# A hybrid decoder layer on one core: eight orders of products in the expert layer, and three smaller reorderings

## The chip, the cores and the metric

One core of one Trainium2 chip. The metric is the device time of the program in microseconds (us); lower is better.

## What the kernel must compute

One decoder layer for 256 tokens of width 1024 in fp32, followed by a final RMSNorm:

```python
for l in range(DEPTH):                       # DEPTH = 1
    h = rmsnorm(x, norm_mix_g[l])
    proj = h @ w_in[l]                       # q, k, v, gu, gv, gate_a, gate_b
    y_a = moba_attention(q, k, v) @ moba_w_proj[l]
    y_b = gmlp_spatial_gating(gu, gv, ...) @ gmlp_w_proj[l]
    x = x + (sigmoid(gate_a) * y_a + sigmoid(gate_b) * y_b) @ w_out[l]
    x = x + memory_cross_attention(rmsnorm(x, norm_xa_g[l]), rmsnorm(mem, norm_mem_g[l]), ...)
    x = x + peer_ffn(rmsnorm(x, norm_ffn_g[l]), w_q, subkeys, w_down, w_up)
return rmsnorm(x, final_g)
```

`peer_ffn` scores each token against 2 x 128 sub-keys for each of 8 heads, takes the best 16 pairs, and adds up, with softmax weights, gelu(h . w_down[e]) * w_up[e] for the experts e that were chosen, out of 128 x 128.

## The kernel before

Every fp32 weight block (128 x 1024) is loaded by SyncE, rounded by ScalarE to a high part `hi` (L140), and the rest, the low part `lw`, is subtracted by VectorE or GpSimd (L142; `lo_engine` says which). Blocks that are listed in `spread` have their subtraction cut into two halves (L146), which are put into a list `half` and emitted where the program calls `half.pop(0)()`. A product is three matmuls: high weights by high data, high weights by low data, low weights by high data (`mm3`, L179 to L181). Loads and conversions run ahead of use: taking a block converts the one two places later.

The order of work on each engine is the order in which the program emits it. The front part runs the mixing block, the cross attention (`xquery`, `xscore`, `xscale`, `xtrans`, `xvalue`; transposes at L641) and its output projection. Then 16 query blocks follow (`for n in range(16)`): each is a `tblock` of 24 matmuls, a copy to `qp`, and one block later `pscore` (L752), a score copy to `S`, and `best`, a round of top-8 operations on VectorE. In the first three of them `pq.add` squares the residual stream on ScalarE and adds up on VectorE (L267); `pq.matmul` (L273) sums over partitions, in the middle of block 3; `newton` makes the third norm's factor, `bcast` spreads it, and `norm_block` normalises one eighth of the data in each of eight blocks.

The expert layer computes all 16,384 experts densely. `down` (128 calls) makes one block of 128 experts' first-layer products, 24 matmuls of 256 columns into the accumulator `A`, and a gelu. VectorE chooses the experts meanwhile (routing: the top-8 rounds and many small operations); one-hot products (`gstep`, tile `m`) then spread the routing weights, and `umm` (L1012 to L1016) multiplies with the second layer's blocks, matmuls of 512 columns. A plan at the top interleaves `down`, `gstep` and `umm`. The final norm squares the accumulators on ScalarE (L1082), forms the factor in small steps, scales on GpSimd (first 128 tokens) or VectorE (last 128) and stores each half row.

Of the kernel before, what the change touches and what calls it, by code (L numbers as in the profile page):

```python
# [16 lines left out]
F32 = mybir.dt.float32  # L17
# [4 lines left out]
AF = mybir.ActivationFunctionType  # L22
OP = mybir.AluOpType
# [3 lines left out]
D = 1024  # L27
S = 256
KD = 8
EPS = 1e-6  # L30
# [15 lines left out]
N_XO, N_PQ = 4, 16  # L46
# [43 lines left out]
def body(tc, I, out, dbg=None):  # L90
# [3 lines left out]
    V, A, P, T, SY = nc.vector, nc.scalar, nc.gpsimd, nc.tensor, nc.sync  # L94
# [10 lines left out]
    nf = I["wf"].shape[0]  # L105
    steps = plan()
    stream = [("f", n) for n in range(nf)] + [x for x in steps if x[0] in "du"]
    raws, convs, later = {}, {}, []
    spread, half = [*range(52, 60), nf - N_PQ - 3, *range(nf - N_PQ - 2, nf - N_PQ + 2)], []
    pos = {"load": 0, "conv": 0, "take": 0}  # L110

    def load_to(n):
        while pos["load"] < min(n, len(stream)):
            m = pos["load"]
            kind, idx = stream[m]
            raw = wst.tile([128, 1024], F32, name="raw", bufs=RAW)
            SY.dma_start(raw, {"f": I["wf"], "d": I["wd"], "u": I["wu"]}[kind][idx])
            raws[m] = raw
            pos["load"] += 1

    def lo_engine(m):
        kind, idx = stream[m]
        if kind == "f":
            return V if idx < nf - N_PQ + 2 else P
        if kind == "d" and idx < FIRST:
            return P
        return V
# [23 lines left out]
    def take(kind):  # L151
        m = pos["take"]
        assert stream[m][0] == kind
        pos["take"] += 1
        conv_to(m + 1 + LEAD)
        load_to(m + 1 + LEAD + RAW)
        for fn in later:
            fn()
        later.clear()
        return convs.pop(m)  # L160


    def sl(k):
        return (slice(None), k, slice(None))

    def tsl(t):
        return slice(t * 128, (t + 1) * 128)
# [9 lines left out]
    def mm3(ps, w, wsl, x, xsl, start, stop):  # L177
        (wh, wl), (xh, xl) = w, x
        T.matmul(ps, wh[wsl], xh[xsl], start=start, stop=False)  # L179
        T.matmul(ps, wh[wsl], xl[xsl], start=False, stop=False)  # L180
        T.matmul(ps, wl[wsl], xh[xsl], start=False, stop=stop)  # L181
# [14 lines left out]
    def mean_sq(v, ms, width):  # L196
        V.tensor_scalar(v, ms, 1.0 / width, EPS, op0=OP.mult, op1=OP.add)
# [5 lines left out]
    mid = ctx.enter_context(tc.tile_pool(name="mid", bufs=1))  # L203
# [10 lines left out]
    def pmm():  # L214
        return pf.tile([128, S], F32, name="mm", bufs=3)
# [7 lines left out]
    xT = fo.tile([128, KD, S], F32, name="xT")  # L223
# [5 lines left out]
    raw0 = wst.tile([128, 1024], F32, name="raw", bufs=RAW)  # L229
    raws[0] = raw0  # L230
    pos["load"] = 1
    for k in range(2):
        SY.dma_start(raw0[:, k * 512:(k + 1) * 512], I["wf"][0][:, k * 512:(k + 1) * 512])
        SY.dma_start(xT[:, k], I["xT"][:, k])
    for j in range(1, 4):
        SY.dma_start(xT[:, 2 * j:2 * j + 2], I["xT"][:, 2 * j:2 * j + 2])
        load_to(j + 1)
    warm = cst.tile([128, 1], F32, name="warm")
    A.activation(warm, ones, AF.Sqrt)
    wps = pat([128, 128])  # L240
# [48 lines left out]
    def tblock(w, x, n=KD, base=0, mid=None):  # L289
        ps = pmm()  # L290
        for k in range(n):
            if mid and k == n // 2:
                mid()
            c = (base + k) * 128
            mm3(ps, w, (slice(None), slice(c, c + 128)), x, sl(k), k == 0, k == n - 1)
        return ps
# [23 lines left out]
    raw0 = raws.pop(0)  # L320
# [7 lines left out]
    for k in range(2):  # L328
        ks = slice(k * 512, (k + 1) * 512)
# [48 lines left out]
    for c in range(4):  # L378
        for nm in ("q", "k"):
            first = c == 0  # L380
            ps = tblock(take("f"), xg, mid=(sqp.matmul if nm == "q" else rope_norm) if first else None)
# [139 lines left out]
    for c in range(4):  # L521
        ps = tblock(take("f"), xg)
# [37 lines left out]
    for c in range(4):  # L560
        ps = tblock(take("f"), mg)
# [42 lines left out]
    pq = Squares(fp2, "x1")  # L604
    for c in range(KD):
        ps = tblock(take("f"), mp)
# [30 lines left out]
    def xtrans(t, h):  # L637
        ps = pat([128, 2, 2, 128])
        for i in range(2):
            for sb in range(2):  # L640
                T.transpose(ps[:, i, sb], Px[t][:, h + i, sb * 128:(sb + 1) * 128], ident)  # L641
        PT = fp2.tile([128, 2, 2, 128], F32, name="PT", bufs=4)
        if t:
            V.tensor_copy(PT, ps)
        else:
            A.copy(PT, ps)
        XT_[t, h] = PT


    def xscale(h):  # L650
        xr = fp2.tile([128, 2], F32, name="xr", bufs=4)
        V.reciprocal(xr, xs[:, :, 2, h])
        for t in range(2):
            V.tensor_scalar(Px[t][:, h], Px[t][:, h], xr[:, t:t + 1], None, op0=OP.mult)
# [26 lines left out]
    xscale(2)  # L681
    xtrans(0, 0)
    xtrans(1, 0)
    skh = [fo.tile([128, 8, 128], F32, name="kT")]
    P.dma_start(skh[0], I["skT"][:, 0:8])
    xscale(3)
    nm_.step()
    V.tensor_scalar(vm[:, 0], nm_.ps[0], rm[:, 0:1], None, op0=OP.mult)
    A.activation(vm[:, 1], nm_.ps[1], AF.Copy, scale=rm[:, 1:2])
# [8 lines left out]
    xg2 = pair("xg", fo)  # L698
    rp = rs1.enter_context(tc.tile_pool(name="route", bufs=2, side="right", reuse_waits="tile"))
    S1 = rp.tile([128, 8, 2, 2, 128], F32, name="S1", bufs=1)  # L700
    x2T = rp.tile([128, KD, S], F32, name="x2T", bufs=1)
    pq = Squares(fp2, "x2")
    for c2 in range(4):
        w = take("f")
        for c in range(2):
            cc = 2 * c2 + c
            ps = tblock(w, oxT, n=4, base=4 * c)
# [30 lines left out]
    h3 = pair("mg", mid)  # L738

    def norm_block(k):  # L740
        hx = fp2.tile([128, S], F32, name="hx", bufs=3)
        V.scalar_tensor_tensor(hx, x2T[:, k], gcol[:, 3, k:k + 1], r3bc, op0=OP.mult, op1=OP.mult)
        later.append(lambda: split(h3[0][:, k], h3[1][:, k], hx))
# [12 lines left out]
    for n in range(16):  # L756
        sk = skh[n // 8][:, n % 8]
        w = take("f")
        if n == 4:
            v3 = fp2.tile([128, 2], F32, name="v3")  # L760
            sq_sum(pq, v3)
        if n == 5:
            r3 = newton(fp2, v3, 2, "r3")
            V.tensor_copy(r3c, r3)
        ps = tblock(w, xg2, mid=pq.matmul if n == 3 else None)
        qp = fp2.tile([128, S], F32, name="qp", bufs=2)
        A.copy(qp, ps)
        qps[n] = (qp, sk)
        if n < 3:
            for k in range(3 * n, min(3 * n + 3, 8)):  # L770
                pq.add(x2T[:, k], A, V)
        if n == 7:
            bcast(r3, r3bc)
            norm_block(0)
        if 8 <= n < 15:
            norm_block(n - 7)
        if n > 0:
            pscore(n - 1)
    pscore(15)
# [6 lines left out]
    gp = g.enter_context(tc.tile_pool(name="exp", bufs=2, reuse_waits="tile"))  # L786
    pp = g.enter_context(tc.tile_pool(name="pexp", bufs=1, space=PSUM, reuse_waits="tile"))
    yps = [[pp.tile([128, 512], F32, name=f"y{t}{z}") for z in range(2)] for t in range(2)]
    Aq = {}

    def mblock():
        return pp.tile([128, 512], F32, name="m", bufs=2)

    def down(i2):
        w = take("d")
        ps = pp.tile([128, S], F32, name="A", bufs=2)
        for k in range(KD):
            mm3(ps, w, (slice(None), slice(k * 128, k * 128 + 128)), h3, sl(k), k == 0, k == KD - 1)
        a = gp.tile([128, S], F32, name="aring", bufs=RING)
        A.activation(a, ps, AF.Gelu_apprx_tanh)  # L800
        Aq[i2] = a
# [76 lines left out]
    n, spent = 0, 0.0  # L878
# [39 lines left out]
    for j in range(3):  # L918
        ps = mblock()[:, :S]
# [11 lines left out]
    for t in range(2):  # L931
        for k in range(KD):
            T.matmul(yps[t][k // 4][:, (k % 4) * 128:(k % 4 + 1) * 128], x2T[:, k, tsl(t)], ident,
                     start=(k % 4 == 0), stop=False, skip_group_check=True)
# [97 lines left out]
    for n, x in enumerate(rest):  # L1032
# [16 lines left out]
        else:  # L1049
            up_a(x[1])  # L1050
            up_b(x[1])
            w = take("u")
# [18 lines left out]
    sqs = wst.tile([128, D], F32, name="raw", bufs=RAW)  # L1071
    for t in range(2):
        ulast(ws, [UP[i2] for i2 in range(128 - TAILN, 128)], t)
        scale = P.tensor_scalar if t == 0 else V.tensor_scalar
        fs = gp.tile([128, 2], F32, name="fs")
        yg = wst.tile([128, D], F32, name="raw", bufs=RAW)
        fm = gp.tile([128, 1], F32, name="fm")
        fv = gp.tile([128, 1], F32, name="fv")
        sq = gp.tile([128, 1], F32, name="fsq")
        for z in range(2):  # L1080
            zs = slice(z * 512, (z + 1) * 512)
            A.activation(sqs[:, zs], yps[t][z], AF.Square, accum_out=fs[:, z:z + 1])  # L1082
            if z == 1:
                V.tensor_add(fm, fs[:, 0:1], fs[:, 1:2])
                mean_sq(fv, fm, D)
                A.activation(sq, fv, AF.Sqrt)
            V.tensor_mul(yg[:, zs], yps[t][z], fg[:, zs])
        fy = gp.tile([128, 1], F32, name="fy")
        V.reciprocal(fy, sq)
        fu = gp.tile([128, 1], F32, name="fu")  # L1090
        V.scalar_tensor_tensor(fu, fy, fy, fv, op0=OP.mult, op1=OP.mult)
        V.tensor_scalar(fu, fu, -0.5, 1.5, op0=OP.mult, op1=OP.add)
        for z in range(2):
            zs = slice(z * 512, (z + 1) * 512)
            scale(yg[:, zs], yg[:, zs], fy, fu, op0=OP.mult, op1=OP.mult)
            (SY if z == 0 or t == 0 else A).dma_start(out[0, tsl(t), zs], yg[:, zs])
    g.close()
    ctx.close()

# [73 lines left out]
```

## Time and profile before

| | us |
|---|---|
| median of 3 runs | 1051.2 (1049.24 to 1052.67) |
| profiled execution, its own time | 1049.31 |
| its span, first to last instruction | 1047.6 |
| TensorE matmuls busy | 1029.6 (98%) |
| VectorE busy | 763.3 (73%) |
| ScalarE busy | 593.9 (57%) |
| GpSimd busy | 63.5 (6%) |
| mean granted TensorE clock | 0.996 of full speed |

Times in the profile count from the span's start. Matmul records overlap, since they are pipelined: the distance from start to start is what one costs, not its own duration. In the profile PE is TensorE, DVE VectorE, ACT ScalarE, POOL GpSimd and SP SyncE.

### The profile page before, as it was taken

To read this page: it belongs to the slowest core of one execution; us is meant where nothing else is said; L and a number is where in the kernel's file an instruction comes from. 1 tells how busy PE (TensorE), PEld (TensorE's weight loads), DVE (VectorE), ACT (ScalarE), POOL (GpSimd) and SP (SyncE) were. 2 spreads that over 40 slices of the span, in tenths; PEclk is the share of its full clock that TensorE was granted. 3 is DMA by queue.
4 is the path that set the end of the run, shared out by engine and by line. 5 is a ranking of instruction groups with operands and counts; after the bars stand their busy time and mean duration, and the time that the engine had idled before them with its cause. 6 is when DMAs were issued, how large, how long until landed. Compare 5 with 4: busy or idle time off the path is not lost.

```text
span 1047.6 us, 19742 instructions
## 1 busy us (share of the span) xinstructions
PE 1029.6 (98%) x7862; PEld 953.1 (91%) x7862; DVE 763.3 (73%) x1502; ACT 593.9 (57%) x935; POOL 63.5 (6%) x53
## 2 busy tenths in 40 slices
PE   9999999998999999999999999999999999999997
PEld 7989999998999999999988998899999988888885
DVE  6765797688999899965656565666799766666666
ACT  6955745665654567755454545454678654444554
POOL 0400000016740000000000000000000000000000
PEclk9999999999999999999999999999999999999999
DMA  8644655554456534456666566656444565656562
GB/s 291 232 138 133 197 173 168 174 164 140 157 165 203 171 118 155 147 180 189 194 188 194 185 198 187 195 185 198 149 157 140 181 192 191 196 188 197 187 198 101
DMA packets 52365, 185.84 MB, mean 177 GB/s; under 512 B 5937, under 2 KB 6833, under 8 KB 52145
## 3 DMA queue, kind: packets, MB, share of 16 engines
q1 hardware_dynamic: 51552, 183.20, 54.6%
q8 instruction: 61, 1.00, 0.4%
q0 software_dynamic: 288, 1.05, 0.3%
q10 hardware_dynamic: 432, 0.34, 0.1%
q14 instruction: 32, 0.25, 0.1%
HBM read 183.52 MB, written 1.05 MB: 176 GB/s over the span
## 4 chain that ended last, share of the span: by engine, by line
PE 89%; DVE 7%; ACT 2%; DMA 1%; issue 1%; DVEq 0%; SPq 0%; ACTq 0%
PE A L179 11%; PE y L1016 11%; PE y L1013 11%; PE y L1012 11%; PE A L181 11%; PE A L180 11%; PE mm L179 5%; PE mm L180 5%; PE mm L181 5%; PE m L985 2%; PE m L984 2%; DVE lw L142 1%; ACT hi L140 1%; DMA raw<-in_wf 1%; PE at L406 1%; PE nat L312 1%
## 5 line engine op out<-in xcount | busy, mean ns | idle before, releaser
L142 DVE TENSOR_TENSOR lw<-raw,hi 128x1024 fp32r<-128x1024 f32 (+1 forms) x309 | 377.1, 1222 | 229.9 <-ACT hi L140 229.0
L140 ACT CAST hi<-raw 128x1024 fp32r<-128x1024 f32 (+1 forms) x341 | 355.4, 1043 | 189.4 <-issue 139.5
L179 PE MATMUL A<-mgh,hi 128*128 128x256 f32 x1024 | 290.2, 283 | 0.0
L181 PE MATMUL A<-mgh,lw 128*128 128x256 f32 x1024 | 287.6, 281 | 1.8 <-DVE lw L142 1.8
L180 PE MATMUL A<-mgl,hi 128*128 128x256 f32 x1024 | 287.4, 281 | 0.0
L181 PEld LDWEIGHTS A<-mgh,lw 128*128 128x128 f32 x1024 | 195.8, 191 | 2.2 <-DVE lw L142 2.2
L1012 PE MATMUL y<-hi,gahl 128*128 128x512 f32 x504 | 196.1, 389 | 0.0
L1013 PE MATMUL y<-lw,gahl 128*128 128x512 f32 x504 | 196.1, 389 | 0.0
L180 PEld LDWEIGHTS A<-mgl,hi 128*128 128x128 f32 x1024 | 192.8, 188 | 2.2
L179 PEld LDWEIGHTS A<-mgh,hi 128*128 128x128 f32 x1024 | 192.3, 188 | 2.2
L1016 PE MATMUL y<-hi,gahl 128*128 128x512 f32 x504 | 155.2, 389 | 0.0
L800 ACT ACTIVATE aring<-A 128x256 f32<-128x256 f32 x128 | 49.2, 384 | 161.7 <-PE A L181 161.7
L179 PE MATMUL mm<-xgh,hi 128*128 128x256 f32 x416 | 119.1, 286 | 0.3 <-DVE q L368 0.3
L181 PE MATMUL mm<-xgh,lw 128*128 128x256 f32 x416 | 116.4, 280 | 0.0
L180 PE MATMUL mm<-xgl,hi 128*128 128x256 f32 x416 | 116.4, 280 | 0.0
L1016 PEld LDWEIGHTS y<-hi,gahl 128*128 128x128 f32 x504 | 94.6, 188 | 19.6
L1012 PEld LDWEIGHTS y<-hi,gahl 128*128 128x128 f32 x504 | 94.6, 188 | 17.4
L1013 PEld LDWEIGHTS y<-lw,gahl 128*128 128x128 f32 x504 | 94.6, 188 | 17.4
L179 PEld LDWEIGHTS mm<-xgh,hi 128*128 128x128 f32 x416 | 79.0, 190 | 1.3 <-issue 0.7
L181 PEld LDWEIGHTS mm<-xgh,lw 128*128 128x128 f32 x416 | 79.1, 190 | 0.0
L180 PEld LDWEIGHTS mm<-xgl,hi 128*128 128x128 f32 x416 | 78.9, 190 | 0.1
L986 ACT ACTIVATE G<-m 128x512 f32<-128x512 f32 x64 | 66.0, 1141 | 5.0 <-PE m L985 2.3
(272 smaller groups left out, 1246.8 us busy)
## 6 DMA issues: line engine op xcount, KB each, us to landing
raw<-in_wd SPq DMA_DIRECT2D x128, 512.0 KB, 3.8
raw<-in_wu SPq DMA_DIRECT2D x128, 512.0 KB, 4.1
raw<-in_wf SPq DMA_DIRECT2D x83, 512.0 KB, 3.7
memT<-in_memT SPq DMA_DIRECT2D x1, 1024.0 KB, 7.3
xT<-in_xT SPq DMA_DIRECT2D x3, 256.0 KB, 6.7
out_y<-raw SPq DMA_DIRECT2D x3, 256.0 KB, 2.0
raw<-in_wf SPq DMA_DIRECT2D x2, 256.0 KB, 3.5
wmT<-in_wsT SPq DMA_DIRECT2D x1, 512.0 KB, 6.2
```

Source lines behind the costliest of these rows:

```text
L140: A.copy(hi[:, ps], raw[:, ps])
L142: lo_engine(m).tensor_sub(lw[:, ps], raw[:, ps], hi[:, ps].bitcast(F32))
L179: T.matmul(ps, wh[wsl], xh[xsl], start=start, stop=False)
L180: T.matmul(ps, wh[wsl], xl[xsl], start=False, stop=False)
L181: T.matmul(ps, wl[wsl], xh[xsl], start=False, stop=stop)
L800: A.activation(a, ps, AF.Gelu_apprx_tanh)
L984: T.matmul(ps[:, t], a1[at], bh[at], start=True, stop=False)
L985: T.matmul(ps[:, t], a1[at], bl[at], start=False, stop=True)
L986: A.activation(Gq[q][:, :, s * TG + c:s * TG + c + 8].rearrange("p i t -> p t i"), ps, AF.Copy, scale=1.0 / 16384.0)
L1012: T.matmul(yps[t][z], gh[:, tsl(t)], wh[:, zs], start=False, stop=False, skip_group_check=True)
L1013: T.matmul(yps[t][z], gh[:, tsl(t)], wl[:, zs], start=False, stop=False, skip_group_check=True)
L1016: T.matmul(yps[t][z], gl[:, tsl(t)], wh[:, zs], start=False, stop=False, skip_group_check=True)
```

## The change

Four edits. `down` takes one of eight orders by block number modulo 8: the old order; low weights first (1); low data first (2); the eight k-tiles backwards (3); the second matmul cut into 240 and 16 columns (4), or into 128 and 128 (5); all products with high weights before all with low (6); even k-tiles, then odd (7). The third norm's squares are spread 4, 3, 1 over the query blocks in place of 3, 3, 2, its column sums stand behind block 3 and not within it, the normalisation starts at block 6 and not 7, and two more low-part subtractions of query blocks go to VectorE; one more block before them is cut in halves, emitted within the cross attention. The first loads go in eight issues and not ten. The final norm forms mean and root in one ScalarE instruction and splits the last scaling between two engines.

```diff
-    spread, half = [*range(52, 60), nf - N_PQ - 3, *range(nf - N_PQ - 2, nf - N_PQ + 2)], []
+    spread, half = [*range(52, 60), nf - N_PQ - 4, nf - N_PQ - 3, *range(nf - N_PQ - 2, nf - N_PQ + 2)], []
...
-            return V if idx < nf - N_PQ + 2 else P
+            return V if idx < nf - N_PQ + 4 else P
...
-    for k in range(2):
-        SY.dma_start(raw0[:, k * 512:(k + 1) * 512], I["wf"][0][:, k * 512:(k + 1) * 512])
-        SY.dma_start(xT[:, k], I["xT"][:, k])
-    for j in range(1, 4):
-        SY.dma_start(xT[:, 2 * j:2 * j + 2], I["xT"][:, 2 * j:2 * j + 2])
-        load_to(j + 1)
+    SY.dma_start(raw0[:, 0:512], I["wf"][0][:, 0:512])
+    SY.dma_start(xT[:, 0:2], I["xT"][:, 0:2])
+    SY.dma_start(raw0[:, 512:1024], I["wf"][0][:, 512:1024])
+    SY.dma_start(xT[:, 2:4], I["xT"][:, 2:4])
+    load_to(2)
+    SY.dma_start(xT[:, 4:8], I["xT"][:, 4:8])
+    load_to(4)
...
     xtrans(1, 0)
+    half.pop(0)()
...
     xscale(3)
+    half.pop(0)()
...
-        ps = tblock(w, xg2, mid=pq.matmul if n == 3 else None)
+        ps = tblock(w, xg2)
...
-        if n < 3:
-            for k in range(3 * n, min(3 * n + 3, 8)):
-                pq.add(x2T[:, k], A, V)
-        if n == 7:
+        for k in ((0, 1, 2, 3), (4, 5, 6), (7,))[n] if n < 3 else ():
+            pq.add(x2T[:, k], A, V)
+        if n == 3:
+            pq.matmul()
+        if n == 6:
             bcast(r3, r3bc)
-            norm_block(0)
-        if 8 <= n < 15:
-            norm_block(n - 7)
+        if 6 <= n < 14:
+            norm_block(n - 6)
...
+    FORMS = 8
+    def passes(form):
+        ks = list(range(KD))
+        tri = [(0, 0), (0, 1), (1, 0)]
+        if form == 1:
+            tri = [(1, 0), (0, 0), (0, 1)]
+        elif form == 2:
+            tri = [(0, 1), (0, 0), (1, 0)]
+        elif form == 3:
+            ks = ks[::-1]
+        elif form == 6:
+            return [(k, 0, x, 0, S) for k in ks for x in (0, 1)] + [(k, 1, 0, 0, S) for k in ks]
+        elif form == 7:
+            ks = ks[::2] + ks[1::2]
+        r = [(k, a, x, 0, S) for k in ks for (a, x) in tri]
+        if form in (4, 5):
+            k, a, x, _, _ = r[1]
+            cut = 240 if form == 4 else 128
+            r[1:2] = [(k, a, x, 0, cut), (k, a, x, cut, S)]
+        return r
...
-        for k in range(KD):
-            mm3(ps, w, (slice(None), slice(k * 128, k * 128 + 128)), h3, sl(k), k == 0, k == KD - 1)
+        order = passes(i2 % FORMS)
+        for n, (k, a, x, c0, c1) in enumerate(order):
+            T.matmul(ps[:, c0:c1], w[a][:, k * 128:(k + 1) * 128], h3[x][:, k, c0:c1], start=n == 0,
+                     stop=n == len(order) - 1)
...
-            A.activation(sqs[:, zs], yps[t][z], AF.Square, accum_out=fs[:, z:z + 1])
-            if z == 1:
-                V.tensor_add(fm, fs[:, 0:1], fs[:, 1:2])
-                mean_sq(fv, fm, D)
-                A.activation(sq, fv, AF.Sqrt)
+            A.activation(sqs[:, zs], yps[t][z], AF.Square, scale=1.0 / 32.0, accum_out=fs[:, z:z + 1])
+            if z == 0:
+                V.tensor_scalar(f0, fs[:, 0:1], EPS, None, op0=OP.add)
+            else:
+                A.activation(sq, fs[:, 1:2], AF.Sqrt, bias=f0)
             V.tensor_mul(yg[:, zs], yps[t][z], fg[:, zs])
+        V.tensor_scalar(fv, fs[:, 1:2], f0, None, op0=OP.add)
...
+            V.tensor_scalar(fr, fu, fy, None, op0=OP.mult)
+            A.activation(yg[:, 0:512], yg[:, 0:512], AF.Copy, scale=fr)
+            V.tensor_scalar(yg[:, 512:], yg[:, 512:], fr, None, op0=OP.mult)
+            SY.dma_start(out[0, tsl(t), 512:], yg[:, 512:])
+            A.dma_start(out[0, tsl(t), 0:512], yg[:, 0:512])
```

## Rows read from the trace of the kernel before

**Rows 1.** Waits of TensorE: total us, times, longest us.

```profile
PE at L273 <- DVE sq L267: 4.2, 1, 4.2
...
PE nat L312 <- ACT hi L140: 1.2, 1, 1.2
...
PE m L921 <- DVE i1T L923: 0.3, 1, 0.3
```

**Rows 2.** Stretches: length, busy us of each engine, granted clock, DMA.

```profile
244.95:248.30 3.35, 3.35 (x18) 3.35 (x18) 2.04 (x15) 0.00 (x0) 0.00 (x0) 0.50 0.40 152
248.60:288.90 40.30, 40.23 (x347) 40.04 (x346) 37.91 (x215) 25.39 (x49) 28.67 (x12) 1.00 0.44 145
288.90:364.60 75.70, 73.87 (x627) 73.47 (x626) 72.95 (x304) 38.76 (x57) 11.06 (x14) 1.00 0.56 179
456.00:741.00 285.00, 285.00 (x1732) 255.92 (x1731) 170.52 (x231) 138.07 (x205) 0.00 (x0) 1.00 0.61 191
```

**Rows 3.** Timeline of VectorE, 231 to 244 us: start, us.

```profile
233.75 7.70 DVE L267 TENSOR_TENSOR sq<-sq 128x256 f32<-128x256 f32 x5 [1.62 <-ACT sq L261]
241.36 0.48 DVE L728 MAX8 M<-S 128x8 f32<-128x128 f32 x2
...
243.71 0.94 DVE L267 TENSOR_TENSOR sq<-sq 128x256 f32<-128x256 f32 x2
```

**Rows 4.** Timeline of GpSimd, 232 to 260 us.

```profile
232.62 4.93 POOL L142 TENSOR_TENSOR lw<-raw,hi 128x1024 fp32r<-128x1024 f32 x2 [12.57 <-ACT hi L140]
238.04 2.59 POOL L142 TENSOR_TENSOR lw<-raw,hi 128x1024 fp32r<-128x1024 f32 x1 [0.48 <-ACT hi L140]
```

**Rows 5.** Timeline of TensorE: first and last of blocks, other shapes.

```profile
104.28 0.28 PE L179 MATMUL mm<-xgh,hi 128*128 128x256 f32 x1
...
107.00 0.28 PE L179 MATMUL mm<-xgh,hi 128*128 128x256 f32 x1
...
216.77 0.94 PE L661 MATMUL mm<-PT,vm 128*128 128x128 f32 x7
...
700.21 0.28 PE L179 MATMUL A<-mgh,hi 128*128 128x256 f32 x1
...
703.04 0.39 PE L1012 MATMUL y<-hi,gahl 128*128 128x512 f32 x1
703.26 0.39 PE L1013 MATMUL y<-lw,gahl 128*128 128x512 f32 x1
```

**Rows 6.** Timeline of TensorE: starts of query blocks 3 and 4.

```profile
238.89 0.36 PE L179 MATMUL mm<-xgh,hi 128*128 128x256 f32 x1
...
248.58 0.36 PE L179 MATMUL mm<-xgh,hi 128*128 128x256 f32 x1
```

**Rows 7.** Timeline of VectorE in the cross attention.

```profile
209.94 1.23 DVE L142 TENSOR_TENSOR lw<-raw,hi 128x1024 fp32r<-128x1024 f32 x1 [1.54 <-ACT hi L140]
211.09 0.69 DVE L629 TENSOR_REDUCE xs<-at 128x2 f32<-128x512 f32 x1
...
212.61 0.68 DVE L644 COPY PT<-at 128x512 f32<-128x512 f32 x1
```

**Rows 8.** Timeline of TensorE in the cross attention.

```profile
213.32 0.44 PE L641 MATMUL at<-ident,Px 128*128 128x128 f32 x2 [0.87 <-DVE PT L644]
213.91 0.88 PE L641 MATMUL at<-ident,Px 128*128 128x128 f32 x6 [0.15 <-DVE Px L654]
```

**Rows 9.** Timeline of all engines at the end.

```profile
1041.41 0.47 DVE L1084 TENSOR_TENSOR fm<-fs 128x1 f32<-128x1 f32 x1 [0.67 <-ACT raw L1082]
...
1041.98 0.68 DVE L1087 TENSOR_TENSOR raw<-y,raw 128x512 f32<-128x512 f32 x1
...
1043.21 1.00 DVE L1095 TENSOR_SCALAR raw<-raw,fy,fu 128x512 f32<-128x512 f32 x2
1044.25 0.35 ACTq L1096 DMA_DIRECT2D out_y<-raw  x1
```

**Rows 10.** Timeline of TensorE behind the routing.

```profile
359.33 0.38 PE L181 MATMUL A<-mgh,lw 128*128 128x256 f32 x1 [1.44 <-DVE lw L142]
```

More of the change, by code (lines that the diff above doesn't have):

```diff
@@ L1073, in body @@
         ulast(ws, [UP[i2] for i2 in range(128 - TAILN, 128)], t)
-        scale = P.tensor_scalar if t == 0 else V.tensor_scalar
         fs = gp.tile([128, 2], F32, name="fs")
         yg = wst.tile([128, D], F32, name="raw", bufs=RAW)
-        fm = gp.tile([128, 1], F32, name="fm")
+        f0 = gp.tile([128, 1], F32, name="fm")
         fv = gp.tile([128, 1], F32, name="fv")
@@ L1092, in body @@
         V.tensor_scalar(fu, fu, -0.5, 1.5, op0=OP.mult, op1=OP.add)
[L1093 to L1096, printed above, removed]
+        if t == 0:
+            for z in range(2):
+                zs = slice(z * 512, (z + 1) * 512)
+                P.tensor_scalar(yg[:, zs], yg[:, zs], fy, fu, op0=OP.mult, op1=OP.mult)
+                SY.dma_start(out[0, tsl(t), zs], yg[:, zs])
+        else:
+            fr = gp.tile([128, 1], F32, name="fr")
+            V.tensor_scalar(fr, fu, fy, None, op0=OP.mult)
[3 more added lines that the diff above has]
+            A.dma_start(out[0, tsl(t), 0:512], yg[:, 0:512])
     g.close()
```

## Prediction

> **What bounds the kernel now.** I read the waits of TensorE first, then the busy time stage by stage, then the timeline of the engines around each edit. In the stage from 456 to 741 us TensorE is busy for all 285 us [rows 2]: there time can only come from a shorter distance between matmuls. Earlier TensorE is almost always busy too, and its own waits are few and can be counted [rows 1]. The longest, 4.2 us, is one instruction, the column sums of the third norm (L273), which wait for VectorE's additions of squares. It costs more than it shows: in the 3.35 us right behind it the granted clock is 0.50, the 1.2 GHz level, and TensorE had stood still before the clock fell [rows 2].
>
> How that wait arises is seen on two engines. VectorE's first five additions take 7.70 us from 233.75 [rows 3], while the last two take 0.94; GpSimd at that time subtracts for two weight blocks, 2.46 us each [rows 4]. So an addition that meets such a subtraction takes as long as it does. Then one round of top-8 operations, 241.36 to 243.71, stands ahead of the last two additions [rows 3]. TensorE meanwhile has half of its fourth query block done and cannot go on.
>
> The last reading is the spacing of the three-product blocks. The same 24 matmuls of 256 columns take 2.72 us from 104.28 to 107.00 and 2.83 us from 700.21 to 703.04 [rows 5]: 0.1133 against 0.118 us each, both at the full clock. No wait lies between them. I take them as two rhythms in which the array can run; every down block that I looked at between 456 and 741 has the slower one.
>
> **The change part by part.** The sum goes against the profiled execution's own 1049.3 us (span 1047.6 and 1.7 around it), which is 1.9 us under the median of the runs shown.
>
> *Third norm.* Query block 4 starts 9.69 us after block 3 (238.89 to 248.58) [rows 6]. After the change block 3 is not interrupted: 24 matmuls at 0.118 are 2.83 us, and four small matmuls for the norm and four for the scores at 0.11 each (the spacing of the 128-column matmuls with full weights [rows 5]) are 0.88. That makes 3.71 us, if the sums are ready, and saves 6.0. Are they? Two more low-part subtractions move from GpSimd to VectorE, 1.2 us each (a whole one is in [rows 7]), and seven additions at about 0.5 no longer meet GpSimd there. VectorE is idle until 233.75, so the first subtraction costs nothing; then six additions at 0.5, the second subtraction of 1.2 and 2.35 of top-8 end at 233.75 + 6.55 = 240.3. The last addition would meet GpSimd's first remaining subtraction (the third of the old order, from 238.04 [rows 4]; 2.4 us without a clash) and end near 240.8. TensorE asks for it only after block 3, at 241.7. Cover 0.9 us: if it is lacking, the addition meets the next subtraction and 1 to 2.4 us of wait come back. I take 6.0, bounds 3.6 and 6.2. The normalisation blocks come one query block earlier; VectorE is relieved at the stage's end by that. From 249 to 364 us VectorE hardly idles (37.9 us of 40.3, then 73.0 of 75.7 [rows 2]), but the work that releases it (the score copies) comes from TensorE, so its routing work begins earlier by the same amount; I expect the 6 us to survive.
>
> *Cross attention.* The subtraction at 209.94 waits for a cast and holds up the softmax reduction behind it on VectorE; at the end of that queue the copy at 212.61 [rows 7] keeps TensorE from its transposes for 0.87 us, and a scaling for 0.15 more [rows 8]. Cut in halves and put behind the transposes, it lets the reduction start 2.7 us earlier. What is late next is the softmax scaling for the last head, after ScalarE's cast, near 211.8, before TensorE is free at 212.3; the two waits and about 0.5 us of copies ahead of the value products go: 1.5 us, bounds 0.5 and 1.7.
>
> *First loads.* Eight issues take the place of ten on SyncE's queue, so the second weight block is issued about one issue earlier; TensorE waits 1.2 us for its conversion [rows 1]. Against that the first x tile arrives with twice the bytes. I take 0.5, bounds -0.3 and 1.2.
>
> *Final norm.* Now the last square sum ends at 1041.4, the mean is formed at 1041.41 to 1042.06, the gain product at 1041.98 stands ahead of the reciprocal, and two scalings end at 1044.2, when ScalarE issues the last store [rows 9]. After: the root follows the square on ScalarE with the bias already formed, the gain product runs meanwhile, the two scalings run on two engines. One more small factor (0.15) is added. By these durations ScalarE's scaling ends near 1043.1 and the store is issued there: 1.1 us, bounds 0.8 and 1.4.
>
> *Orders.* Six of the eight issue the same 24 matmuls; I give the reordering itself no price, since a weight load stands before every matmul as before. Two of them (32 blocks of the 128) issue a 25th, with its own weight load. Below: nothing, as 512 columns take 0.22 us, twice a 256-column matmul [rows 5], if only columns count. Above: a whole further 0.118. Matmuls of 128 columns with 128x128 weights stand at 0.11 us though they stream half the columns [rows 5], so a weight load binds them; I take 0.11 for both cuts, 32 x 0.11 = 3.5 us, range 0 to 3.8. Six of those blocks lie ahead of the wait of 1.44 us at 359.33 for a low part that VectorE makes after its routing work [rows 10]; that wait covers 0.6, which leaves 2.9.
> The Trainium skill (TensorE: Matmul & The Clock Gate, Back-to-back issue gap) gives an isolated gap of columns / 2.4 + 2.5 ns; by it a cut block costs an estimated 2.5 ns more, 0.1 us in all, and the whole change would come out near 2.8 us better than my sum. The same page (LDWEIGHTS) puts a load at columns / 1.2, 107 ns for 128; the trace's 0.11 us sides with that.
>
> The rhythm may change too. One block costs 2.83 - 2.72 = 0.11 us more in the slow one; all 128 would give about 14. A cut matmul breaks the regular alternation of loads and columns, as other small matmuls do, after which I found either rhythm, the slow one more often. I count 14 blocks' worth, 1.5 us, as a choice; bounds 0 and 12.
>
> Sum: 6.0 + 1.5 + 0.5 + 1.1 - 2.9 + 1.5 = 7.7 us less: 1041.6 on the profiled execution's scale, 1043.5 against the median.
>
> **Rivals.**
> *A, the orders free most blocks of the slow rhythm.* For: two rhythms exist with the same tiles, so addresses alone don't set it. Against: the rhythm lasts through changes of tile and through 512-column blocks. Two thirds of the 128 blocks give 9 us instead of 1.5: 1036.
> *B, the third norm still waits.* The last addition meets GpSimd's second subtraction and ends 2.4 us later; TensorE stands for 1.6 to 2 us and perhaps loses clock again. For: the cover is only 0.9 us. Against: two subtractions have left GpSimd. Gain 5 to 6: 1046.
> The Trainium skill (SBUF — State Buffer, Who interferes with whom) says that a VectorE instruction with two SBUF inputs and a GpSimd instruction that reads SBUF exclude each other for the whole instruction. The stretched additions agree.
> *C, the orders cost more than nothing (the other side).* An order may fit loads and columns together worse than the old one: the loads and matmuls are of equal length here, so a few ns per pair are open. The other parts give 9.1 and the cuts take 2.9. Break-even is at 6.2 us over 3072 matmuls, 2.0 ns each, or 16 ns if only one order in eight is affected. At 4 ns on all the time is 1057; at 2 ns, no change. Against: of the products' operands none changes its place.
> *D, the norm's gain is given back* to VectorE's routing work, which has 5 us idle in all from 249 to 364 [rows 2]: then 6 us shrink to 2 and the time is 1047.5 to 1049. Against: TensorE's wait for the routing's result is 0.3 us [rows 1].
>
> **How the numbers follow.** My forecast 0.50, A 0.20, B 0.12, C 0.11, D 0.07. Within 0.3% means 1048.0 to 1054.4, about what a measurement here can tell. The forecast is faster in nearly all its range (its own: 1040 to 1047.5, from the cuts at nothing to the norm at its lower bound), A always; B mostly; D half; C half slower, half same. Faster 0.78, same 0.15, slower 0.07. The range leaves out the far half of A and most of C and of D: 1036 to 1050.
>
> **What would show it.** No wait at L273 above 1 us and no stretch at clock 0.5 near 245; query blocks at an even 3.2 to 3.3 us; transposes of the cross attention without a 0.9 us wait; some 1.1 us less between the last matmul and the last store; blocks with a 25th matmul 0.1 us longer than their neighbours; down blocks mostly at 2.83, some at 2.72 us. I am wrong if an order has a spacing of its own above 0.118, if more than half of the blocks run at 0.1133, or if TensorE waits for low parts (L142) grow between 280 and 360 us by as much as the norm gave.

## The result, and the profile after

The changed kernel takes 1042.6 us (median of four runs, 1041.16 to 1044.13) against 1051.1 (four runs, 1049.24 to 1052.67): ratio 0.992, interval 0.990 to 0.994. The forecast was 1043.5, with a range of 1036 to 1050. The profiled execution of after took 1044.13 us (span 1042.4), the slowest of its four, so the pair of profiles differs by 5.2 us and the medians by 8.5. Before's profiled execution lies 1.8 us under its median and after's 1.5 over; both are within the scatter of single executions, and no trace shows where those 3.3 us lie.

Where the 5.2 us lie is read by following the same matmuls through both traces: the start of one after, less its start before, is what has been gained up to there.

| up to the start of | before | after | gained so far | in this stage |
|---|---|---|---|---|
| first weight block with 256 columns (L179) | 19.01 | 19.27 | -0.3 | -0.3 |
| last projection block of the cross attention | 200.14 | 201.19 | -1.1 | -0.8 |
| output projection of the cross attention | 218.70 | 217.83 | 0.9 | 1.9 |
| query block 3 | 238.89 | 238.05 | 0.8 | 0.0 |
| query block 4 | 248.58 | 241.77 | 6.8 | 6.0 |
| first `down` block | 288.91 | 282.19 | 6.7 | -0.1 |
| `down` block 24 | 357.50 | 349.39 | 8.1 | 1.4 |
| `down` block 27 | 373.17 | 367.37 | 5.8 | -2.3 |
| last matmul | 1040.20 | 1035.54 | 4.7 | -1.1 |
| issue of the last store | 1044.25 | 1039.05 | 5.2 | 0.5 |

One edit is seen at once, the third norm. The rest are one to two us each, of both signs. The 0.8 us ahead of the cross attention's last projection block lie in seven blocks that took 2.83 us and not 2.72, in a part that the change doesn't touch.

The waits of TensorE after [rows 1] no longer have the column sums among their long ones. The longest is now one for a low part behind the routing:

```profile
PE A L825 <- DVE lw L142: 2.4, 2, 2.1
PE nat L313 <- ACT xgh L170: 1.0, 1, 1.0
...
PE nat L313 <- ACT hi L140: 0.5, 1, 0.5
PE at L642 <- ACT Px L633: 0.4, 1, 0.4
```

The timeline of VectorE after, in the cross attention [rows 7] and ahead of the third norm's sums [rows 3]:

```profile
209.38 0.69 DVE L630 TENSOR_REDUCE xs<-at 128x2 f32<-128x512 f32 x1
...
210.90 0.69 DVE L645 COPY PT<-at 128x512 f32<-128x512 f32 x1
211.50 0.69 DVE L146 TENSOR_TENSOR lw<-raw,hi 128x512 fp32r<-128x512 f32 x1
...
231.73 1.23 DVE L142 TENSOR_TENSOR lw<-raw,hi 128x1024 fp32r<-128x1024 f32 x1 [0.45 <-ACT hi L140]
232.90 1.49 DVE L268 TENSOR_TENSOR sq<-sq 128x256 f32<-128x256 f32 x3
234.45 1.23 DVE L142 TENSOR_TENSOR lw<-raw,hi 128x1024 fp32r<-128x1024 f32 x1
235.59 1.48 DVE L268 TENSOR_TENSOR sq<-sq 128x256 f32<-128x256 f32 x3
236.99 0.48 DVE L731 MAX8 M<-S 128x8 f32<-128x128 f32 x2
...
239.34 0.55 DVE L268 TENSOR_TENSOR sq<-sq 128x256 f32<-128x256 f32 x1
```

And that of GpSimd [rows 4]:

```profile
237.21 2.39 POOL L142 TENSOR_TENSOR lw<-raw,hi 128x1024 fp32r<-128x1024 f32 x1 [18.02 <-ACT hi L140]
239.86 2.37 POOL L142 TENSOR_TENSOR lw<-raw,hi 128x1024 fp32r<-128x1024 f32 x1 [0.27 <-ACT hi L140]
```

Six additions take 2.97 us where five took 7.70. GpSimd starts when they are done; the seventh begins at 239.34, 0.26 us before the end of the first subtraction, takes 0.55 and ends at 239.9. The reader should now find the same places on TensorE: the transposes [rows 8], the query blocks [rows 6], the matmul behind the routing [rows 10], and two `down` blocks between 512-column products, one with a cut (form 4) and one without (form 6) [rows 5]:

```profile
213.35 1.04 PE L642 MATMUL at<-ident,Px 128*128 128x128 f32 x8
214.24 0.49 PE L662 MATMUL mm<-PT,vm 128*128 128x128 f32 x2
...
238.05 0.36 PE L179 MATMUL mm<-xgh,hi 128*128 128x256 f32 x1
...
240.96 0.50 PE L274 MATMUL at<-ones,sq 128*128 128x1 f32 x4
...
241.77 0.36 PE L179 MATMUL mm<-xgh,hi 128*128 128x256 f32 x1
...
351.89 0.39 PE L825 MATMUL A<-mgh,lw 128*128 128x256 f32 x1 [2.11 <-DVE lw L142]
...
473.39 0.28 PE L825 MATMUL A<-mgh,hi 128*128 128x256 f32 x1
473.51 0.29 PE L825 MATMUL A<-mgl,hi 128*128 128x240 f32 x2
473.65 0.36 PE L825 MATMUL A<-mgh,lw 128*128 128x256 f32 x1
...
476.02 0.28 PE L825 MATMUL A<-mgl,hi 128*128 128x256 f32 x1
476.14 0.28 PE L825 MATMUL A<-mgh,lw 128*128 128x256 f32 x1
476.25 0.39 PE L1040 MATMUL y<-hi,gahl 128*128 128x512 f32 x1
...
487.30 0.28 PE L825 MATMUL A<-mgh,hi 128*128 128x256 f32 x1
...
490.12 0.39 PE L1040 MATMUL y<-hi,gahl 128*128 128x512 f32 x1
```

Query block 4 follows block 3 after 3.72 us, where it was 9.69; the sums start at 240.96, right behind the last product, 1.1 us after their last addition. The wait behind the routing has grown from 1.44 to 2.11 us. The cut block lasts 2.86 us and the uncut one 2.82. The windows show what follows the longer wait (its granted clock, third value from the end, is 0.50), and the long stage in the middle:

```profile
353.36:356.77 3.41, 3.41 (x18) 3.41 (x18) 0.74 (x1) 0.98 (x2) 0.00 (x0) 0.50 0.96 300
443.00:736.30 293.30, 293.30 (x1788) 263.23 (x1788) 176.29 (x238) 142.38 (x213) 0.00 (x0) 1.00 0.58 190
```

The same stage, from the start of block 48 to that of block 90, lasted from 448.85 to 741.65, 292.8 us, before: half a us less. At last the end [rows 9], all engines:

```profile
1036.69 0.69 DVE L1114 TENSOR_TENSOR raw<-y,raw 128x512 f32<-128x512 f32 x1 [0.61 <-ACT raw L1109]
1036.69 0.29 ACT L1113 ACTIVATE fsq<-fs,fm 128x1 f32<-128x1 f32 x1
...
1038.30 0.72 ACT L1129 ACTIVATE raw<-raw,fr 128x512 f32<-128x512 f32 x1 [1.31 <-DVE fr L1128]
1038.30 0.49 DVE L1130 TENSOR_SCALAR raw<-raw,fr 128x512 f32<-128x512 f32 x1
...
1039.05 0.35 ACTq L1132 DMA_DIRECT2D out_y<-raw  x1
```

The two scalings do run side by side, but the gain product starts only when ScalarE's square of the same accumulator has ended.

### The profile page after: what moved, and what is told of

Same layout as the page of the kernel before. It is cut to its first block, busy times and chain, and to the rows that moved or that the text cites. A ratio compares the mean times of both kernels' runs of the same rounds, so it can differ in the third digit from the quotient of the medians.

```text
span 1042.4 us, 19809 instructions
## 1 busy us (share of the span) xinstructions
PE 1029.4 (99%) x7894; PEld 953.4 (91%) x7894; DVE 760.3 (73%) x1505; ACT 594.6 (57%) x936; POOL 58.3 (6%) x51
## 4 chain that ended last, share of the span: by engine, by line
PE 88%; DVE 8%; ACT 1%; DMA 1%; issue 1%; DVEq 0%; ACTq 0%
PE A L825 28%; PE y L1041 11%; PE y L1040 11%; PE y L1044 11%; PE mm L179 6%; PE mm L180 6%; PE mm L181 6%; DVE lw L142 3%; PE m L1013 2%; PE m L1012 1%; DVE jk L875 1%; DMA raw<-in_wf 1%; DVE acc L865 1%; PE nat L313 1%; PE nat L315 1%
## 5 line engine op out<-in xcount | busy, mean ns | idle before, releaser
L825 PE MATMUL A<-mgh,hi 128*128 128x256 f32 x1024 | 283.6, 282 | 0.0
L825 PE MATMUL A<-mgl,hi 128*128 128x256 f32 (+2 forms) x1056 | 281.8, 278 | 0.0
L825 PE MATMUL A<-mgh,lw 128*128 128x256 f32 x1024 | 270.0, 282 | 2.4 <-DVE lw L142 2.4
L825 PEld LDWEIGHTS A<-mgl,hi 128*128 128x128 f32 x1056 | 197.1, 189 | 1.9
L825 PEld LDWEIGHTS A<-mgh,lw 128*128 128x128 f32 x1024 | 186.3, 190 | 3.1 <-DVE lw L142 2.8
L179 PE MATMUL mm<-xgh,hi 128*128 128x256 f32 x416 | 118.4, 285 | 0.3 <-DVE q L369 0.3
L1044 PEld LDWEIGHTS y<-hi,gahl 128*128 128x128 f32 x504 | 94.6, 188 | 19.7
L179 PEld LDWEIGHTS mm<-xgh,hi 128*128 128x128 f32 x416 | 78.4, 188 | 1.3 <-issue 0.7
```

The costliest lines, as they stand in the source:

```text
L825: T.matmul(ps[:, c0:c1], w[a][:, k * 128:(k + 1) * 128], h3[x][:, k, c0:c1], start=n == 0, stop=n == len(order) - 1)
L1044: T.matmul(yps[t][z], gl[:, tsl(t)], wh[:, zs], start=False, stop=False, skip_group_check=True)
```

## Experiments

Times are medians; ratios are to the kernel before in the same batch, with 95% intervals. "After with" starts from the changed kernel, "before with" from the old one.

**The eight orders.** The first question was whether the gain needs the orders at all. First, after with the old order in every block:

```diff
-    FORMS = 8
+    FORMS = 1
```

> The changed kernel with the old order in all 128 down blocks; the other three edits stay. Theory 1 (the orders give nothing net: a cut block costs 0.11 us, wins back 0.08 to 0.10 in its own later matmuls and loses the quicker rhythm at the next 512-column block; in the routing stage the quicker blocks only wait longer for a low part): 1 to 2 us faster than the changed kernel, near 1041, and the clock stays at 1.00 behind the routing. Theory 2 (part of the gain comes from the orders): 2 to 4 us slower than the changed kernel, near 1045.5.

Measured: 1041.9 us, 0.9907 (0.9894 to 0.9920). All of the gain is there without the orders. One thing was missed: the half-clock stretch was expected to go, but TensorE waited 2.7 us behind the routing and ran 3.41 us at clock 0.50 from 350.91. The blocks ahead of the wait (6 to 23) had fallen into the quick spacing, 2.72 us each, without any cut.

Next, before with `passes` and the new `down`, and nothing else of the change:

> The kernel before with only the eight orders put in. Theory 1: 0 to 2 us slower than before, near 1052. Theory 2: 2 to 4 us faster than before, near 1048.

Measured: 1052.4 us, 1.0004 (0.9991 to 1.0017). The orders alone are neither a gain nor a loss that can be told: by the interval at most 1 us of the one and 1.8 of the other.

Third, after with all orders but without the two cuts:

```diff
-        if form in (4, 5):
+        if False:
```

> The changed kernel with six of the eight orders: where a matmul was cut, the old order stands, and every block has 24 matmuls. Theory 1 (only a cut changes the rhythm, the sequence of products does not): within 1 us of the kernel without any orders, and blocks of all orders at 2.83 us between 512-column blocks. Rival (the sequence itself sets the rhythm): blocks of one order differ from the others by 0.05 us or more, and the time moves by 2 us or more.

Measured: 1041.8 us, 0.9908 (0.9894 to 0.9921), the same as with one order (the two stood in one batch). Between 512-column products the blocks of all orders take 2.83 us here, so the sequence of the products by itself changes nothing that shows. What the 32 cuts cost is not settled by this time: against the change (0.992) it is 1.3 us by ratio, with intervals that leave room for nothing and for the 2.9 us net of the forecast. The run with the orders alone, cuts included, speaks against 2.9.

**The third norm.** Before with the norm's edits alone:

```diff
-            return V if idx < nf - N_PQ + 2 else P
+            return V if idx < nf - N_PQ + 4 else P
...
-        ps = tblock(w, xg2, mid=pq.matmul if n == 3 else None)
+        ps = tblock(w, xg2)
...
+        for k in ((0, 1, 2, 3), (4, 5, 6), (7,))[n] if n < 3 else ():
+            pq.add(x2T[:, k], A, V)
+        if n == 3:
+            pq.matmul()
```

(with the normalisation from block 6 on, as in the change)

> The kernel before with only the third norm's edit: squares 4, 3, 1, column sums behind block 3, normalisation one block earlier, two more low-part subtractions on VectorE. Theory 1 (the wait and the lowered clock behind it are worth 6.0 us and come through to the end): 1045, 5 to 6.5 us faster than before, no wait above 0.5 us at the column sums. Rival (VectorE's routing work gives it back): 2 us faster or less, 1049.

Measured: 1045.4 us, 0.9941 (0.9925 to 0.9956), which is 6.2 us (0.0059 x 1052). TensorE waits at no column sum; behind the routing it waits 2.7 us, and 3.41 us at half clock follow from 351.38, and still the gain is whole.

Which of the norm's edits carries it? After with one order, and the two subtractions back on GpSimd:

```diff
-            return V if idx < nf - N_PQ + 4 else P
+            return V if idx < nf - N_PQ + 2 else P
```

> The changed kernel without the eight orders, and with the two low-part subtractions of the third norm's edit left on GpSimd; squares, column sums and normalisation stay in their new order. Theory 1 (an addition that meets a GpSimd subtraction lasts until that one ends, so the move to VectorE is what makes the sums ready in time): additions of 1.5 to 2.4 us come back, the last one ends 2 to 4 us later than in the changed kernel, TensorE waits 1 to 3 us at the column sums, and the time is 1.5 to 5 us above the kernel without the orders. Rival (the later place of the column sums alone is enough): no wait there above 0.5 us and no difference of 1 us.

Measured: 1050.0 us, 0.9994 (0.9985 to 1.0003). The whole gain of the change is gone, not only the norm's, and the rows say how. Waits of TensorE, VectorE's additions, GpSimd's subtractions:

```profile
PE at L274 <- DVE sq L268: 5.2, 1, 5.2
PE A L825 <- DVE lw L142: 3.1, 2, 2.7
```

```profile
233.20 10.66 DVE L268 TENSOR_TENSOR sq<-sq 128x256 f32<-128x256 f32 x6 [1.62 <-ACT sq L262]
...
246.12 0.41 DVE L268 TENSOR_TENSOR sq<-sq 128x256 f32<-128x256 f32 x1
```

```profile
232.08 2.41 POOL L142 TENSOR_TENSOR lw<-raw,hi 128x1024 fp32r<-128x1024 f32 x1 [12.58 <-ACT hi L140]
...
240.16 2.36 POOL L142 TENSOR_TENSOR lw<-raw,hi 128x1024 fp32r<-128x1024 f32 x1 [0.27 <-ACT hi L140]
```

Six additions take 10.66 us. Four of them meet one of four subtractions that follow each other; they last 1.6 to 2.6 us, and each ends 0.3 us after its subtraction. The other two come behind GpSimd's fourth subtraction, which ends at 242.52, and take 0.4 each; in after all six take 2.97. The top-8 round that follows pushes the last addition to 246.12. TensorE waits 5.2 us and runs at half clock for 6.83 us from 246.34: more than the wait of 1 to 3 us and the loss of 1.5 to 5 that were expected. Behind the routing it waited 2.7 us in this execution too, and there the clock stayed at 1.00.

The same from the other side: before with that one character.

```diff
-            return V if idx < nf - N_PQ + 2 else P
+            return V if idx < nf - N_PQ + 4 else P
```

> The kernel before with one word's worth of change: two more low-part subtractions of the query blocks go to VectorE and not to GpSimd; squares, column sums and normalisation stay where they were. Theory 1 (the additions were stretched by GpSimd's subtractions, and that is nearly all of the wait): the additions take about 0.5 us each; the last two squares come after one round of top-8 operations, so the column sums in the middle of block 3 wait about 1 us or less, no half clock; 4.5 to 6 us faster than before, near 1046. Rival (the new places of squares and column sums carry the gain): 2 us faster or less.

Measured: 1045.7 us, 0.9946 (0.9932 to 0.9960), 5.7 us. Its additions take 0.4 us (one 0.80), and the wait for them, with the sums still in the middle of block 3, is 0.8:

```profile
PE at L273 <- DVE sq L267: 0.8, 1, 0.8
```

No half clock follows. The character carries nearly all of the norm's gain. The half us by which the whole edit is ahead is well within the intervals, and without the character the new places of squares, sums and normalisation gained nothing (0.9994 above).

**Behind the routing.** The wait in `down` block 24 and the half clock behind it looked like 3 to 4 us to be had. After with one order, and the low part of that block made by GpSimd:

```diff
-        if kind == "d" and idx < FIRST:
+        if kind == "d" and (idx < FIRST or idx == 24):
```

> The changed kernel without the eight orders, and with the low part of down block 24, the one that TensorE waits for behind the routing, subtracted by GpSimd and not by VectorE. Theory 1 (that wait of 2 to 2.7 us and the half clock behind it, 3.4 us long, are on the path that sets the end): the wait falls below 0.5 us, no stretch of half clock before the end, 3 to 4 us faster than the kernel without the orders, near 1038.5. Rival (the routing's result is late anyway, so that TensorE waits at the transposes of the result): the wait moves there and less than 1 us is won.

Measured: 1039.9 us, 0.9897 (0.9882 to 0.9912). Against 0.9907 for the same kernel without it, this is 1 us by ratio and 2 by medians of two batches, less than expected and, with intervals of about 1.5 us either way, not clear of noise. The waits of TensorE say why:

```profile
PE A L825 <- DVE lw L142: 1.4, 2, 1.0
...
PE A L825 <- POOL lw L142: 0.9, 1, 0.9
```

The 2.7 us and the half clock are gone, but two shorter waits, for the next low parts, have come.

**The two spacings.** In after every block with a cut, between 512-column products, lasts 2.86 us, and every other 2.83. Inside the cut block the gaps up to the third product are 0.110, 0.032 and 0.203 us (form 4) or 0.061, 0.113 and 0.171 (form 5) in place of two of 0.118, so the cut costs 0.11; the remaining matmuls then follow at 0.113. If the cut starts the quick spacing and 512 columns end it, one cut should serve several `down` blocks that follow each other. To see this, `down` blocks stand in groups of four between the second layer's, with one order and the first loads as before:

```diff
-        want = (n + 1) * want_end // QI
+        want = want_end if n == QI - 1 else (n + 1) * want_end // QI // 4 * 4
...
+        want = want if want == left else want // 4 * 4
```

> No eight orders, the first loads as before the change, and the down blocks between the second-layer blocks put together in groups of four; no cut. Theory 1 (after 512-column matmuls the slower rhythm holds until something breaks it): each of the four at 2.83 us, time within 1 us of the kernel without the orders; weight block 0's matmuls start 0.2 to 0.4 us earlier than in the changed kernel. Rival (the rhythm is set anew at each block): quicker blocks inside the groups, 1 us faster or more.

And the same with a cut in the first block of each group:

```diff
+    lead = {b[1] for a, b in zip(steps, steps[1:]) if a[0] == "u" and b[0] == "d"}
...
-        order = passes(i2 % FORMS)
+        order = passes(5 if i2 in lead else 0)
```

> As the grouped kernel, and the second matmul of the first block of each group is cut into 128 and 128 columns (13 or 14 more matmuls in all). Theory 1 (a cut starts the quicker rhythm and it lasts through further 256-column blocks, until 512-column matmuls come): the first block of a group 2.86 us, the next three 2.72, and about 0.3 us for each group, 3 to 4 us in all, faster than the grouped kernel without the cut. Rival (the rhythm falls back by itself): the later blocks at 2.83 and 0.5 us slower than the grouped kernel.

Measured: 1041.0 us without, 0.9911 (0.9896 to 0.9926), and 1038.0 with the cuts, 0.9875 (0.9860 to 0.9890); 2.9 us between the medians and 3.8 by ratio, in one batch. TensorE's timeline, one group without a cut (the starts of its first three blocks and of what follows the fourth):

```profile
493.25 0.28 PE L825 MATMUL A<-mgh,hi 128*128 128x256 f32 x1
...
496.08 0.28 PE L825 MATMUL A<-mgh,hi 128*128 128x256 f32 x1
...
498.90 0.28 PE L825 MATMUL A<-mgh,hi 128*128 128x256 f32 x1
...
504.56 0.39 PE L1040 MATMUL y<-hi,gahl 128*128 128x512 f32 x1
```

and one with a cut in its first block:

```profile
490.84 0.28 PE L825 MATMUL A<-mgh,hi 128*128 128x256 f32 x1
490.95 0.34 PE L825 MATMUL A<-mgl,hi 128*128 128x128 f32 x2
...
493.69 0.28 PE L825 MATMUL A<-mgh,hi 128*128 128x256 f32 x1
...
496.41 0.28 PE L825 MATMUL A<-mgh,hi 128*128 128x256 f32 x1
...
499.13 0.28 PE L825 MATMUL A<-mgh,hi 128*128 128x256 f32 x1
...
501.85 0.39 PE L1040 MATMUL y<-hi,gahl 128*128 128x512 f32 x1
```

Four blocks take 11.31 us without and 11.01 with: 2.85, then 2.72 three times. All 13 full groups with a cut do the same. The cut costs its 0.11 and more than pays it back where quick blocks follow.

TensorE's waits for low parts, the longest of them behind the routing, with the cuts:

```profile
PE A L825 <- DVE lw L143: 3.1, 2, 2.7
```

It is the same wait as without them (2.7 us too), but the clock fell behind it for 3.41 us in the execution without cuts and stayed at 1.00 in the one with them. That is not where the 2.9 us come from: the mean clock of all executions is 0.997 to 0.999 without the cuts and 0.997 to 0.998 with them, and the groups differ row by row.

**The cross attention.** Before with the subtraction in halves and nothing else:

```diff
-    spread, half = [*range(52, 60), nf - N_PQ - 3, *range(nf - N_PQ - 2, nf - N_PQ + 2)], []
+    spread, half = [*range(52, 60), nf - N_PQ - 4, nf - N_PQ - 3, *range(nf - N_PQ - 2, nf - N_PQ + 2)], []
...
     xtrans(1, 0)
+    half.pop(0)()
...
     xscale(3)
+    half.pop(0)()
```

> The kernel before with only the cross attention's edit (one more block's low part in halves behind the transposes). Theory 1: the wait of 0.87 us at the transposes is gone and the value products start 1.5 to 2 us earlier; 1.5 to 2 us faster than before, near 1049.5. Rival (given back at the third norm, where VectorE is late): less than 0.7 us, as the wait at the column sums grows by what was won.

Measured: 1049.7 us, 0.9984 (0.9974 to 0.9994), 1.7 us. The wait for `PT` is gone, and the waits further on are still there, the one behind the routing (2.7 us) longer than the 1.44 of before:

```profile
PE A L181 <- DVE lw L142: 3.1, 2, 2.7
...
PE at L273 <- DVE sq L267: 4.1, 1, 4.1
```

Half clock follows both (6.83 us from 242.45, 3.41 us from 358.50).

**The parts together.** The grouped kernel with cuts and block 24's low part on GpSimd (the edits of the experiments above):

> The edits that the runs so far speak for: third norm, cross attention and final norm as changed, first loads as before, no eight orders, down blocks in groups of four with the first of each group cut, and the low part of down block 24 on GpSimd. Theory 1: the gains add up, 3 to 5 us faster than the changed kernel, 1037 to 1038. Rival (GpSimd's subtraction and the cut groups gain the same microsecond): no faster than the grouped and cut kernel, 1038 to 1039.

Measured: 1036.4 us, 0.9862 (0.9843 to 0.9881), the fastest of all: 14.7 us less than the kernel before in its batch, and about 6 less than the change.

## Why the prediction came out right, step by step

**Third norm: 6.0 forecast, 6.0 measured**, between the two query blocks, and 6.2 by itself. The mechanism is the one that the prediction read from [rows 3, 4]: an addition that meets a subtraction on GpSimd takes as long as it does. Moving two subtractions away takes the stretching away, moving them back restores it, and with it the wait and the half clock. The Trainium skill (SBUF — State Buffer, Who interferes with whom) says that a VectorE instruction with two SBUF inputs and a GpSimd instruction that reads SBUF exclude each other. The traces agree: six additions took 10.66 us beside GpSimd and 2.97 without. The order of events came as worked out and a little earlier: the last addition ended at 239.9 and not 240.8, its cover was 1.1 us and not 0.9. Rival B needed it to end 2.4 us later and fails. What the forecast did not see is how few of the edits are needed: it reckoned the saving as that of an uninterrupted block 3, but with the sums still inside it 5.7 of the 6.2 us come (4.2 to 7.1 by the interval).

**Cross attention: 1.5 forecast, 1.9 in the pair, 1.7 by itself** (0.6 to 2.7 by the interval). The copy that held the transposes now starts at 210.90 and not 212.61, and the waits of 0.87 and 0.15 are gone. A wait of 0.4 for ScalarE (L642), 3 us earlier, stood before as well. The softmax scaling that was named as next holds nothing up: the eight transposes follow each other from 213.35. The 1.9 lies 0.2 us above the upper bound of 1.7, less than the interval of the run tells apart.

**First loads: 0.5 forecast, -0.3 in the pair.** What was set against the gain came: TensorE's first product with a loaded weight block starts at 4.95 to 5.33 us in the eight traces with the old loads and at 6.48 to 6.83 in the five with the new, since the first x tile lands later: ScalarE starts on it at 5.92 us in after and at 4.77 before. Most of it is made up by the first block at L179: 18.7 to 19.4 us (20.5 in one execution that was at half clock there) against 19.0 to 19.7. No run had the loads as its only difference, so what they are worth at the end stays open; no trace shows the half us of gain.

**Final norm: 1.1 forecast, 0.54 measured; this term was mis-sized.** The step that failed is "the gain product runs meanwhile": it waits 0.61 us for ScalarE's square (1036.69 above), which reads the same accumulator. Between the last matmul and the issue of the last store lie 4.04 to 4.05 us in all five traces with the old final norm and 3.50 to 3.51 in all eight with the new. That the two read one accumulator is shown; whether the wait is a need of the chip or a dependency of the program is open.

**Cuts and rhythm: +2.9 and -1.5 forecast, together a loss of 1.4; by the runs nothing that can be measured** (1.0004 for the orders alone, and 0.9907 and 0.9908 without orders or without cuts, against 0.992). The price of a cut was right: 0.11 us, a whole weight load, where columns alone would make it nothing. The estimate of 2.5 ns a cut, from the gap of an isolated matmul in the Trainium skill (TensorE: Matmul & The Clock Gate, Back-to-back issue gap), does not fit the 0.11 us. The 107 ns for a load of 128 columns by the Trainium skill (TensorE: Matmul & The Clock Gate, LDWEIGHTS) does. But the two terms are one and were wrongly added up as if apart: a cut block pays 0.11 and then runs quick, so alone it costs 0.03 (and not the 0.1 that the prediction gave as a sign), 0.8 us for some 25 of them in the pair (-1.1 was measured from block 27 on). The prediction had the quick spacing as a matter of chance (14 blocks); in the `down` blocks it follows a cut without exception between 512-column products (among the one-hot products two of the twelve cut blocks, 93 and 108, stayed slow). Its reading that a rhythm lasts through 512-column blocks held for the slow one alone.

Where no such product stood, in blocks 4 to 23, the blocks were quick from the first cut up to the wait: 1.4 us in the pair. That gain can't be credited to the cuts: of the eleven traces without a cut in those blocks eight have blocks 6 to 23 quick behind a wait of 0.4 us in block 5, one has only the first of them quick, and two (before, and the one character alone) are slow behind the same wait. And most of it goes into the wait behind the routing: where the blocks were slow, TensorE waited 1.4 us there, where they were quick without a cut 2.7 (with block 24's low part still on VectorE). In the pair TensorE came 8.1 us earlier to block 24 and VectorE's low part 7.4 earlier (359.33 to 351.89), so the wait grew by 0.7; 3.41 us at half clock, worth 1.7 us of full speed, came after it: 2.3 us given back. Taking the wait away with block 24's low part on GpSimd gave only 1 to 2 us, in which the next low parts, late too, have their share.

**The rivals.** A (the orders free most blocks) and C (they cost more) both fall with 1.0004: by its interval the orders are worth no more than 1 us and cost no more than 1.8. A's mechanism was half there, in the cut alone, and shows when the blocks are grouped. D (the gain is given back to VectorE's routing) falls too: with the norm's edits alone 6.2 us arrive at the end, though the wait behind the routing grew there as well.

That the sum of 7.7 stands so near 8.5 owes something to cancellation: the norm and the cross attention gave 7.9 by themselves, the final norm half of its term, the first loads show no gain, and the orders took nothing that can be measured where a net loss of 1.4 was put down.

## What to carry to other kernels

When a short VectorE instruction with two SBUF inputs takes several times its usual time, look at what GpSimd is doing at that moment: here moving two subtractions onto the busier engine was worth 5.7 us, because 1.2 us on VectorE replaced 2.4 us on GpSimd that held up VectorE as well. Before adding an instruction to break a pattern, see how long the benefit lasts: a cut that costs one weight load pays when several blocks of the same shape follow, and not when each block gets its own. And a wait taken away early is worth what the next late buffer lets through; follow the same instruction through both traces, stage by stage, to see where a gain goes.

## What was not expected of the hardware

The two spacings of 256-column products with full weight loads, 0.113 and 0.118 us at the same granted clock, can be chosen in the stage with 512-column products: one product cut in two starts the quick one, 512-column products end it, and it lasts through at least three further blocks of 24 (2.72 us each). Blocks between 512-column products were at 2.83 in the old order and in each of the five other uncut ones. What in the array makes the two spacings stays open.

The clock fell behind some of TensorE's waits and not behind others. At the column sums of the third norm it fell for 3.41 to 6.83 us behind waits of 3.7 to 5.2 us, and not behind one of 0.8. Behind the routing it fell for 3.41 us behind waits of 2.11 to 2.73 us in six traces and not behind waits of 2.72 and 2.73 us in two others (the subtractions back on GpSimd, and the groups with cuts); behind the waits of 1.4 us in three traces it never fell. So the same wait came with and without the lower clock here, and what decides it stays open. In the pair a wait that grew by 0.7 us, from 1.44 to 2.11, cost 2.3 us because the clock did fall.
